# Six buffers for the first modulation rows, and weight sums moved ahead in a bidirectional scan layer

## The chip, the cores and the metric

The kernel runs on one core of a Trainium2 chip. The metric is the device time of one execution, in microseconds (us); each time shown is a median of several executions. Shares and rows come from one execution that the hardware profiler took.

## The reference

One layer of a diffusion backbone over 2176 tokens of width 1024: 128 context tokens and 2048 latent tokens, with different modulation vectors. The layer is, for both groups:

```python
mod = silu(c) @ w_mod + b_mod                       # 6 x 1024: shift1, scale1, gate1, shift2, scale2, gate2
h = rmsnorm(x, norm1) * (1 + scale1) + shift1
z = h @ w_in                                        # sc_b, sc_c, sc_x | q, k, v, o | gates
y_sc = sc_b * conv3(sc_c * sc_x)                    # short convolution, 512 wide
h_m = mlstm_bidir(q, k, v, gates, C0, n0, m0)       # 4 heads of 128, chunks of 128 tokens, both directions
h_m = headnorm(h_m) * sigmoid(o)
x = x + gate1 * (concat([y_sc, h_m]) @ w_out)
h2 = rmsnorm(x, norm2) * (1 + scale2) + shift2
a, g = split(conv3(h2 @ w_up))                      # 2 x 2816
x = x + gate2 * ((silu(g) * a) @ w_down)
y = rmsnorm(x, final_norm)
```

All arrays are float32. The kernel returns `y` for all tokens and the final scan states of the context tokens.

## The kernel before

Activations lie transposed: 128 features on the partitions, tokens along the free axis. A projection in float32 precision is made of three matmuls in a reduced format: each operand is split in a high part (made by ACT) and a low part (made by DVE as the rest), `wh`/`wl` for weights, `hH`/`hL` for activations, and `wh*hH`, `wh*hL`, `wl*hH` are added up in one PSUM bank. TensorE (PE) does the matmuls, ACT and DVE split operands and empty PSUM, and SyncE (SP) issues all transfers on one queue, in order. A scheduler puts the instructions of each engine in a fixed order, from the order in which the code is written and its own costs; pools of buffers (`bufs=n`) bound how far a load may run ahead. Each engine executes its own list in order.

The stages, in order of time:

1. First modulation. `mod_pe` loads one 128-wide row of `w_mod` (0.5 MB) and multiplies it with `silu(c)` on PE, 16 times: 8 rows of shift1 and 8 of scale1, in the order scale, shift, scale, shift. The rows go through two buffers `wst` and two `wsu`. Between them `raws(0)` loads the first 512-token block of x, and its squares are summed.
2. Values and gates of the last 1024 tokens (`vg_of`), whose normalized form is `gapply` (scale on DVE, shift and high part on ACT, low part on DVE). Each value weight is loaded through `wst` and split. Then the keys of these tokens (`key`), and `gsums`, which makes sums of activation quarters.
3. The pairs: the other projections of the last 1024 tokens, as ten 2x2 block products with seven products in place of eight (`pair_weights` makes the sums of weights, `pair` does 7 x 12 matmuls). After each of the seven products a generator is stepped (`side`); here that is `first_stats`, the sums of squares of the first 1152 tokens.
4. Values, gates and keys of the first 1152 tokens (`vg_first`, `heads`), and the scan's gate phase between the heads.
5. Scan sums. 34 units `Sums`, one for each chunk and pair of heads: two transposes of `k2` into `S`, a copy to `kT`, two matmuls `vw`x`kT` into `y`, and the running state `sb` from it by ACT and DVE. `weave` puts them between the heads of the projections q and o (`fill`).
6. The scan proper (`Mix`) with the short convolution and the output projection (`out_proj`) between, then the feed-forward layer: seven-product blocks over `w_up` and `w_down`.

Two pieces of work on DVE are put beside stages 4 and 5 as the generator `side`. `prep_down` loads blocks of `w_down`, makes the four sums that the last layer's seven products need, and stores them in `wD`: 12 steps of two loads, four operations and four stores. `mod_dve` computes the 32 other modulation rows on DVE, two reductions of 1024 columns for each. Both use the pool `wm`, four buffers. `side` is stepped once for each step of `vg_first`, of `heads`, and of the weave of the scan sums.

Buffers that the change touches: the pool `rp` (eight buffers of 384 columns, named `row`) takes evicted projection rows and the x rows that `out_proj` adds to; six more of 512 columns in the pool `sw` serve the pairs. The pool `xg` holds x of the second 512-token block and the values on their way out. In the order of instructions below a name ends in the number of its buffer.

Of the kernel before, what the change touches and what calls it, by code (L numbers as in the profile page):

```python
# [58 lines left out]
def hymba_kernel(ctx: ExitStack, tc: tile.TileContext, I, O):  # L59
# [302 lines left out]
    with ExitStack() as ph1:  # L362
# [5 lines left out]
        rp = ph1.enter_context(tc.tile_pool(name="rp", bufs=8))  # L368
# [36 lines left out]
        def head(w, b, h, hs, dst, func, scale):  # L405
            t0, n = BL[b]
            acc = gemm(w, hs[b], n)
            r = rp.tile([P, 384], F32, name="row")
# [68 lines left out]
        def out_proj(defer):  # L477
            def load_r(x):
                m, b = STEPS[x]
                t0, n = BL[b]  # L480
                xr = rp.tile([P, 384], F32, name="row")
                Q.dma_start(xr[:, :n], I["x"][m][:, t0:t0 + n])
                return xr
# [63 lines left out]
        with tc.tile_pool(name="ex", bufs=1, side="right") as ex, \  # L547
# [16 lines left out]
            def raws(blk):  # L564
                def get(pool, name, k0, n, bufs, w):
                    t = pool.tile([P, 4, 384] if w else [P, n, NG], F32, name=name, bufs=bufs)
# [75 lines left out]
            mods(2, 5)  # L642
            inv_rms(ss, NG, gcol(0))
            mods(5, 8)
            ws = load_vg(0)
# [26 lines left out]
            def key(w, h, blk):  # L672
# [24 lines left out]

            def row():
                return sw.tile([P, NG], F32, name="row", bufs=6)
# [178 lines left out]
        def prep_down():  # L878

            for mp in range(4):  # L880
                for c0 in range(0, KD, 512):
                    n = min(512, KD - c0)
                    a, b, s = (mp_.tile([P, 1024], F32, name="wm", bufs=4).rearrange("p (k c) -> p k c", k=2)[:, :, :n]
                               for _ in range(3))
                    for r, t in enumerate((a, b)):
                        Q.dma_start(t, I["w_down"][mp][:, r, :, c0:c0 + n])
                    yield
                    a11, a12, a21, a22 = a[:, 0], a[:, 1], b[:, 0], b[:, 1]
                    V.tensor_add(s[:, 0], a21, a22)
                    V.tensor_sub(s[:, 1], s[:, 0], a11)  # L890
                    V.tensor_sub(a12, a12, s[:, 1])
                    V.tensor_sub(a21, a11, a21)
                    for i, t in enumerate((s[:, 0], s[:, 1], a12, a21)):
                        Q.dma_start(wD[mp, i][:, c0:c0 + n], t)
                    yield

        side = chain(prep_down(), mod_dve())
# [277 lines left out]
        def weave(units, fill, blocks, side=None):  # L1175

            n = len(units)
            for i in range(-1, n + 3):
# [6 lines left out]
                for x in (0, 1) if i < 0 else (i + 2,):  # L1185
# [4 lines left out]
                if side:  # L1190
# [8 lines left out]
        for _ in vg_first():  # L1199
            next(third, None)  # L1200
            next(side, None)
        run(third)
        with tc.tile_pool(name="gt", bufs=1, side="right") as gt:
            gph = gate_phase()
            kh = heads(BA, hs, 16, kD, AF.Copy, 1.0)
            while True:
# [5 lines left out]
                run(islice(kh, 2), side)  # L1212
            run(kh, side)
# [387 lines left out]
```

## Time and profile before

| | |
|---|---|
| median of 3 runs | 2499.48 us (2497.95 to 2500.31) |
| profiled execution | 2498.36 us |
| its span, first to last instruction | 2496.4 us |
| PE busy | 2433.0 us (97%) |
| DVE busy | 1808.2 us (72%) |
| ACT busy | 1143.5 us (46%) |
| mean granted TensorE clock | 0.988 |
| DMA | 506.07 MB, mean 203 GB/s |

A row of the profile names the line, the engine, the operation, what is written and read, and its busy time; the time in brackets is how long the engine sat idle before it and which event ended that. PE is matmul time, PEld the weight loads that overlap it. Tables by stretch give the busy time of each engine in that stretch of the span, the granted clock as a share of full speed, the share of time in which DMA engines were busy, and GB/s. In a profile a buffer's number is left out, so `k2` reads `k`.

### The profile page before, as it was taken

What the parts mean: (1) busy time and instruction counts of PE and PEld (TensorE: products, weight loads), DVE (VectorE), ACT (ScalarE), POOL (GpSimd) and SP (SyncE); (2) the same over time, 40 slices, a digit from 0 to 9 for tenths busy, and PEclk for the clock granted to TensorE, in tenths of its full rate; (3) what the DMA queues carried; (4) which work ended last, traced back from release to release, by engine and by line L of the source; (5) the groups of instructions that cost most, each with busy time, mean ns of one, the idle gap of its engine ahead of it and who ended that gap; (6) DMA issues with size and microseconds to landing.
All of it is one profiled execution on the core that took longest, in us unless ns stands there. A gap on an engine that the chain in (4) does not pass through costs nothing.

```text
span 2496.4 us, 42843 instructions
## 1 busy us (share of the span) xinstructions
PE 2433.0 (97%) x16347; PEld 2325.2 (93%) x16347; DVE 1808.2 (72%) x3419; ACT 1143.5 (46%) x2170; POOL 66.7 (3%) x127
## 2 busy tenths in 40 slices
PE   7999999899999989999999999999999999999998
PEld 7988889788999989989999999999999988889998
DVE  4655675687566876789888888776767688677665
ACT  4533453233444543555455446554545454443343
POOL 0000000000011110000000000000000000000000
PEclk9999999899999999999999999999999999999999
DMA  7433169898866886877455446544444476576544
GB/s 268 140 108 116 60 196 306 275 295 275 249 196 211 272 275 201 276 248 254 156 189 210 155 146 229 199 147 168 147 169 146 164 277 231 190 276 204 180 156 149
DMA packets 250270, 506.07 MB, mean 203 GB/s; under 512 B 22850, under 2 KB 145874, under 8 KB 239186
## 3 DMA queue, kind: packets, MB, share of 16 engines
q1 hardware_dynamic: 250066, 503.35, 60.8%
q8 instruction: 128, 2.10, 0.3%
q14 instruction: 76, 0.62, 0.1%
HBM read 355.24 MB, written 148.03 MB: 202 GB/s over the span
## 4 chain that ended last, share of the span: by engine, by line
PE 57%; DMA 4%; DVE 4%; issue 1%; ACT 1%; SPq 0%; POOL 0%; DVEq 0%; ACTq 0%
PE pa L1440 7%; PE pa L1442 7%; PE pa L1441 7%; PE pb L1442 3%; PE pb L1440 3%; PE pb L1441 3%; PE pa L1498 2%; PE pa L1499 2%; PE pa L1500 2%; PE pc L1441 2%; PE pc L1442 2%; PE pc L1440 2%; PE pc L1498 2%; PE pc L1500 2%; PE pc L1499 2%; PE pb L1499 2%
## 5 line engine op out<-in xcount | busy, mean ns | idle before, releaser
L1440 PE MATMUL pa<-tH,wh 128*128 128x272 f32 x1408 | 409.1, 291 | 5.3 <-DVE row L499 4.2
L1442 PE MATMUL pa<-tH,wl 128*128 128x272 f32 x1408 | 407.9, 290 | 0.0
L1441 PE MATMUL pa<-tL,wh 128*128 128x272 f32 x1408 | 406.0, 288 | 0.3 <-DVE tL L280 0.3
L286 ACT ACTIVATE wh<-st 128x512 fp32r<-128x512 f32 (+1 forms) x312 | 189.4, 609 | 408.7 <-PE pa L1441 115.4
L213 PE MATMUL acc<-hH,wh 128*128 128x384 f32 (+1 forms) x960 | 329.4, 343 | 6.3 <-ACT wh L112 6.3
L215 PE MATMUL acc<-hH,wl 128*128 128x384 f32 (+1 forms) x960 | 322.9, 337 | 0.3 <-DVE wl L115 0.2
L214 PE MATMUL acc<-hL,wh 128*128 128x384 f32 (+1 forms) x960 | 322.9, 336 | 0.0
L287 DVE TENSOR_TENSOR wl<-st,wh 128x512 fp32r<-128x512 f32 (+1 forms) x312 | 205.3, 660 | 93.6 <-ACT wh L286 89.4
L1281 DVE SCALAR_TENSOR_TENSOR tt<-raw,fw,tt 128x127 f32<-128x127 f32 (+4 forms) x264 | 242.2, 947 | 41.9 <-ACT tt L1287 40.7
L1440 PEld LDWEIGHTS pa<-tH,wh 128*128 128x128 f32 x1408 | 265.7, 189 | 6.2 <-DVE row L499 4.2
L1441 PEld LDWEIGHTS pa<-tL,wh 128*128 128x128 f32 x1408 | 266.2, 189 | 0.5 <-DVE tL L280 0.5
L1442 PEld LDWEIGHTS pa<-tH,wl 128*128 128x128 f32 x1408 | 265.5, 189 | 0.0
L1440 PE MATMUL pb<-tH,wh 128*128 128x272 f32 x704 | 203.7, 289 | 0.4 <-ACT wh L286 0.4
L1442 PE MATMUL pb<-tH,wl 128*128 128x272 f32 x704 | 203.6, 289 | 0.0
L1441 PE MATMUL pb<-tL,wh 128*128 128x272 f32 x704 | 202.8, 288 | 0.0
L213 PEld LDWEIGHTS acc<-hH,wh 128*128 128x128 f32 x960 | 183.0, 191 | 9.2 <-ACT wh L112 8.4
L215 PEld LDWEIGHTS acc<-hH,wl 128*128 128x128 f32 x960 | 182.1, 190 | 1.9 <-DVE wl L115 1.2
L214 PEld LDWEIGHTS acc<-hL,wh 128*128 128x128 f32 x960 | 183.0, 191 | 0.7 <-issue 0.2
L286 ACT ACTIVATE wh<-s 128x512 fp32r<-128x512 f32 x176 | 110.9, 630 | 150.9 <-PE pc L1441 90.3
L287 DVE TENSOR_TENSOR wl<-s,wh 128x512 fp32r<-128x512 f32 x176 | 120.6, 686 | 33.1 <-ACT wh L286 29.3
L1440 PEld LDWEIGHTS pb<-tH,wh 128*128 128x128 f32 x704 | 132.4, 188 | 0.6 <-ACT wh L286 0.6
L1441 PEld LDWEIGHTS pb<-tL,wh 128*128 128x128 f32 x704 | 132.6, 188 | 0.0
(296 smaller groups left out, 5924.5 us busy)
## 6 DMA issues: line engine op xcount, KB each, us to landing
st<-in_w_up SPq DMA_DIRECT2D x88, 512.0 KB, 4.6
wU<-s SPq DMA_DIRECT2D x22, 1024.0 KB, 7.0
s<-wU SPq DMA_DIRECT2D x22, 1024.0 KB, 5.9
st<-wD SPq DMA_DIRECT2D x32, 704.0 KB, 4.9
st<-in_w_down SPq DMA_DIRECT2D x28, 704.0 KB, 5.3
wst<-in_w_in SPq DMA_DIRECT2D x38, 512.0 KB, 5.1
R<-nD SPq DMA_DIRECT2D x34, 512.0 KB, 5.6
wm<-in_w_modr SPq DMA_DIRECT2D x32, 512.0 KB, 5.1
```

The costliest lines, as they stand in the source:

```text
L213: PE.matmul(acc[:, :n], w_h, hH[:, k, :n], start=(k == 0), stop=False)
L214: PE.matmul(acc[:, :n], w_h, hL[:, k, :n], start=False, stop=False)
L215: mm = PE.matmul(acc[:, :n], w_l, hH[:, k, :n], start=False, stop=(k == KT - 1))
L286: S.activation(wh[:, :n], a, AF.Copy)
L287: V.tensor_sub(wl[:, :n], a, wh[:, :n].bitcast(F32))
L1281: V.scalar_tensor_tensor(o, i, w, o, op0=ALU.mult, op1=ALU.add)
L1440: PE.matmul(acc, wh[:, w], rh, start=(kk == 0 and i in (0, 1, 5)), stop=False, skip_group_check=True)
L1441: PE.matmul(acc, wh[:, w], rl, start=False, stop=False, skip_group_check=True)
L1442: mm = PE.matmul(acc, wl[:, w], rh, start=False, stop=(kk == 3), skip_group_check=True)
L1498: PE.matmul(acc[p], wh[:, k], th[:, t], start=(c == kk == 0), stop=False, skip_group_check=True)
L1499: PE.matmul(acc[p], wh[:, k], tl[:, t], start=False, stop=False, skip_group_check=True)
L1500: PE.matmul(acc[p], wl[:, k], th[:, t], start=False, stop=(c == 2 and kk == nk - 1), skip_group_check=True)
```

## The change

- The first modulation rows go through six buffers in turn, two `wsu` and the four of `xg`; `wst` is left to the value weights, of which the first two are loaded and split between the rows. The second x block is loaded into `xg` after the rows; the last two k-tiles of the first block have a buffer `xh` of their own.
- `prep_down` moves beside the pairs, with three buffers `wm` in the pool `sw` and its sums in a buffer `xt`; it is spread over four steps of `side` for each block. `side` is stepped after every product of the pairs.
- `mod_dve` alone is left beside stages 4 and 5, and is stepped on every second step.
- The scan sums' loads stand three units ahead in the code (two before).
- `row` is one pool for all its users: six buffers of 512 columns. A key is evicted and stored in one piece of 512 columns, not two of 256.

```diff
+    def row():
+        return rp.tile([P, 512], F32, name="row")
...
-        rp = ph1.enter_context(tc.tile_pool(name="rp", bufs=8))
+        rp = ph1.enter_context(tc.tile_pool(name="rp", bufs=6))
...
-                    return get(xp, "xt", 0, 3, 2, 1) + get(xp, "xt", 3, 3, 2, 1) + get(xg, "xg", 6, 2, 5, 0)
-                return [x for k in range(0, KT, 2) for x in get(xg, "xg", k, 2, 5, 0)]
+                    return get(xp, "xt", 0, 3, 2) + get(xp, "xt", 3, 3, 2) + get(xg, "xh", 6, 2, 1)
+                return [x for k in range(0, KT, 2) for x in get(xg, "xg", k, 2, 4)]
...
+            homes6 = cycle("uuxxxx")
+
             def mod_pe(mt):
-                if mt < 8:
-                    st = wp.tile([P, WN], F32, name="wst", bufs=2)
+                if next(homes6) == "u":
+                    st = ex.tile([P, WN], F32, name="wsu", bufs=2)
                 else:
-                    st = ex.tile([P, WN], F32, name="wsu", bufs=2)
+                    st = xg.tile([P, 2, NG], F32, name="xg", bufs=4).rearrange("p k t -> p (k t)")
...
-            mods(2, 5)
+            mods(2, 4)
+            ws = load_vg(0)
             inv_rms(ss, NG, gcol(0))
-            mods(5, 8)
-            ws = load_vg(0)
+            mods(4, 8)
             run(gapply(0, x1))
...
-                for i in range(2):
-                    r = rp.tile([P, 384], F32, name="row")[:, :256]
-                    S.activation(r, acc[:, i * 256:(i + 1) * 256], AF.Copy)
-                    Q.dma_start(kD[h][:, TG + blk * NG + i * 256:TG + blk * NG + (i + 1) * 256], r)
+                r = row()
+                S.activation(r, acc, AF.Copy)
+                Q.dma_start(kD[h][:, TG + blk * NG:TG + (blk + 1) * NG], r)
...
-            side = first_stats()
+            side = chain(first_stats(), prep_down())
             for x, p in enumerate(PAIRS):
                 if x < len(PAIRS) - 1:
-                    run(gpair(*p), side if x > 2 else None, 3)
+                    run(gpair(*p), side)
...
-        side = chain(prep_down(), mod_dve())
+        side = mod_dve()
...
-        for _ in vg_first():
+        for x, _ in enumerate(vg_first()):
             next(third, None)
-            next(side, None)
+            if x % 2:
+                next(side, None)
...
-                for x in (0, 1) if i < 0 else (i + 2,):
+                for x in range(lead) if i < 0 else (i + lead,):
...
-                if side:
+                if side and i % 2:
                     next(side, None)
...
-        weave([Sums(c, hp) for c in range(NL - 1, -2, -1) for hp in range(2)], fill, (1, 0, 1), side)
+        weave([Sums(c, hp) for c in range(NL - 1, -2, -1) for hp in range(2)], fill, (1, 0, 1), 3, side)
```

`prep_down` in its new place, with a pause between its two halves and an empty step behind them:

```python
def prep_down():
    for mp in range(4):
        for c0 in range(0, KD, 512):
            n = min(512, KD - c0)
            a, b = (sw.tile([P, 1024], F32, name="wm", bufs=3).rearrange("p (k c) -> p k c", k=2)[:, :, :n]
                    for _ in range(2))
            s = xp.tile([P, 4, 384], F32, name="xt").rearrange("p k t -> p (k t)")[:, :2 * n]
            ...
            yield
            ...                                      # two sums into s
            yield
            ...                                      # two sums in place, four stores to wD
            yield
            yield
```

The first place is SP's list in the first modulation. Before, from the first x block on (`wsu`, `wst`: rows of `w_mod`; `xt`, `xg_210`: x of the first block; `xg_458`: of the second):

```order
L568 DMA xt_206<-in_x 128x3x512
L568 DMA xt_208<-in_x 128x3x512
L568 DMA xg_210<-in_x 128x2x512
L620 DMA wsu_235<-in_w_mod 128x1024
L620 DMA wst_247<-in_w_mod 128x1024
L620 DMA wsu_260<-in_w_mod 128x1024
L620 DMA wst_272<-in_w_mod 128x1024
L648 DMA bgate_132<-in_b_gate 128x16
L568 DMA xg_458<-in_x 128x2x512
L620 DMA wsu_285<-in_w_mod 128x1024
```

After, from the same place (`xg_235` and the like are rows of `w_mod` now, `wst` the value weights):

```order
L571 DMA xt_206<-in_x 128x3x512
L571 DMA xt_208<-in_x 128x3x512
L571 DMA xh_210<-in_x 128x2x512
L625 DMA xg_235<-in_w_mod 128x1024
L625 DMA xg_247<-in_w_mod 128x1024
L625 DMA wsu_260<-in_w_mod 128x1024
L625 DMA wsu_272<-in_w_mod 128x1024
L110 DMA wst_285<-in_w_vg 128x1056
L110 DMA wst_292<-in_w_vg 128x1056
L625 DMA xg_306<-in_w_mod 128x1024
```

Two value weights come in between the rows, and the second block's x goes behind the last row.

The second place is SP's list at the first loads of the scan sums (`k2`, `v2`). Before, they follow the last stores of keys (`kD`) and of the down weights' sums (`wD`):

```order
L410 DMA kD_63<-row_4227 128x384
L410 DMA kD_63<-row_4262 128x384
L868 DMA wm_4039<-in_w_modr 128x1024
L894 DMA wD_76<-wm_3902 128x384 x2
L894 DMA wD_76<-wm_3900 128x384
L894 DMA wD_76<-wm_3901 128x384
L1036 DMA k2_4277<-kD_63 128x2x128
L1041 DMA v2_4279<-vD_66 128x258
L1036 DMA k2_4281<-kD_63 128x2x128
```

After, they stand among the stores of the values (`vD`) of the stage before, ahead of all stores of keys of the first 1152 tokens:

```order
L403 DMA vD_66<-rv_3412 128x258
L1223 DMA sb_4314<-in_state 128x2x129
L1041 DMA k2_4316<-kD_63 128x2x128
L1046 DMA v2_4318<-vD_66 128x258
L892 DMA wm_3528<-in_w_modr 128x1024
L403 DMA vD_66<-rv_3445 128x258
L1041 DMA k2_4320<-kD_63 128x2x128
L1046 DMA v2_4322<-vD_66 128x258
L1041 DMA k2_4324<-kD_63 128x2x128
```

The loads moved ahead by the whole stage of keys, and the down weights' stores are gone from it.

The third place is DVE's list in the pairs, between two half weights (`wl`). Before, at the second pair's convolution:

```order
L729 TENSOR_TENSOR wl_1575<-wsu_1324,wh_1574 128x512
L798 SCALAR_TENSOR_TENSOR yr_1496<-row_1474,scw_133,yr_1496 128x8x63
L800 SCALAR_TENSOR_TENSOR yr_1496<-row_1474,scw_133,yr_1496 128x8x63
L729 TENSOR_TENSOR wl_1596<-wst_1476,wh_1595 128x512
L722 TENSOR_TENSOR wst_1476<-wst_1476,wsu_1477 128x512
```

After, at the same convolution (`wm`, `xt`: the down weights and their sums, lines 852 to 856):

```order
L730 TENSOR_TENSOR wl_1668<-wsu_1303,wh_1667 128x512
L801 SCALAR_TENSOR_TENSOR yr_1571<-row_1543,scw_133,yr_1571 128x8x63
L717 TENSOR_TENSOR s_1689<-wsu_1552 128x512
L852 TENSOR_TENSOR xt_1664<-wm_1663 128x512
L719 TENSOR_TENSOR s_1689<-s_1689,wst_1551 128x512
L853 TENSOR_TENSOR xt_1664<-xt_1664,wm_1662 128x512
L730 TENSOR_TENSOR wl_1691<-wst_1551,wh_1690 128x512
L855 TENSOR_TENSOR wm_1662<-wm_1662,xt_1664 128x512
L856 TENSOR_TENSOR wm_1663<-wm_1662,wm_1663 128x512
```

The four sums of a down block stand between the pair's own sums and the low parts of its weights.

More of the change, by code (lines that the diff above doesn't have):

```diff
@@ L480, in load_r @@
                 t0, n = BL[b]
-                xr = rp.tile([P, 384], F32, name="row")
+                xr = row()
                 Q.dma_start(xr[:, :n], I["x"][m][:, t0:t0 + n])
@@ L876, in mod_dve @@
                 yield
[L878 to L895, printed above, removed]
-        side = chain(prep_down(), mod_dve())
+        side = mod_dve()
         WG, EM, AC = range(3)
@@ L1173, in third, with weave @@
                 Q.dma_start(yD[4 + 2 * hp:6 + 2 * hp, :, t0:t0 + P].rearrange("h d t -> d h t"), o2)
-        def weave(units, fill, blocks, side=None):
+        def weave(units, fill, blocks, lead, side=None):
             n = len(units)
@@ L1211, in hymba_kernel @@
                     break
-                run(islice(kh, 2), side)
-            run(kh, side)
+                run(islice(kh, 2), side, 2)
+            run(kh, side, 2)
         sbs, sfs = [], []
@@ L1243, in hymba_kernel @@
             sfs.append(sf)
-        weave([Mix(c, hp) for c in range(-1, NL) for hp in range(2)], fill, (2, 1, 2))
+        weave([Mix(c, hp) for c in range(-1, NL) for hp in range(2)], fill, (2, 1, 2), 2)
         phr.close()
```

26 lines of the change are left out of this document (21 added, 5 removed).

## The prediction

> **What bounds the kernel now.** I read the page's first lines, then the busy time by stretch, then each stretch in which TensorE (PE) is not full, in order of time.
>
> ```profile
> span 2496.4 us, 42843 instructions
> ...
> PE 2433.0 (97%) x16347; PEld 2325.2 (93%) x16347; DVE 1808.2 (72%) x3419; ACT 1143.5 (46%) x2170; POOL 66.7 (3%) x127
> ```
>
> PE is busy 97% of the span, so only the 63 us in which it idles, and the stretches at a lower clock, can be won. The next view gives stretches of the span in us: length, busy time of each engine, granted clock, DMA share.
>
> ```profile
> core 0: us, PE busy (x) PEld busy (x) DVE busy (x) ACT busy (x) POOL busy (x), PEclk, DMA share, GB/s
> 0.00:43.03 43.03, 34.11 (x266) 33.82 (x267) 11.69 (x37) 9.41 (x16) 1.40 (x9) 0.96 0.86 302
> 43.03:61.60 18.57, 14.29 (x97) 13.80 (x96) 16.59 (x28) 15.02 (x25) 0.00 (x0) 0.82 0.60 200
> 131.00:330.00 199.00, 199.00 (x874) 162.14 (x873) 114.59 (x183) 74.78 (x133) 3.31 (x3) 1.00 0.28 93
> 352.00:400.00 48.00, 47.34 (x381) 46.93 (x382) 30.75 (x77) 19.58 (x40) 1.43 (x14) 1.00 0.88 291
> 400.00:457.70 57.70, 54.97 (x308) 51.69 (x306) 31.82 (x93) 17.98 (x35) 0.00 (x0) 0.97 0.90 299
> 457.70:478.30 20.60, 10.83 (x29) 8.24 (x30) 14.84 (x30) 3.32 (x8) 0.00 (x0) 0.59 0.87 271
> 478.30:628.80 150.50, 140.27 (x754) 129.56 (x753) 119.20 (x253) 51.06 (x133) 0.00 (x0) 0.98 0.91 280
> 628.80:1070.00 441.20, 433.54 (x2796) 431.69 (x2795) 314.64 (x909) 199.91 (x535) 47.44 (x72) 0.99 0.76 242
> 1100.00:2480.00 1380.00, 1377.36 (x10066) 1336.30 (x10065) 1060.00 (x1630) 682.30 (x1110) 7.51 (x8) 1.00 0.55 189
> ```
>
> In order: the modulation rows; the first value and gate matmuls up to their first eviction; the seven-product pairs (PE full, DMA a quarter busy); the first blocks' values and gates; the keys; the scan sums, as two rows; the scan proper with the output projection; the feed-forward layer. From 628.80 on the order of PE's matmuls is the same in both kernels but for two transposes, and PE is 98% busy or more, so I take the change to act only before 628.80. There PE is short in two places: the first 62 us, and 457.70 to 628.80, where DMA is 0.87 to 0.91 busy.
>
> **First modulation rows.** The rows are from the order of instructions by time: start, duration, and in brackets the idle time and its releaser. One row of `w_mod` is 16 records.
>
> ```profile
> 13.54 1.95 PE L623 MATMUL acc<-csil,wst 128*128 128x128 f32 x16
> ...
> 17.64 3.59 PE L623 MATMUL acc<-csil,wsu 128*128 128x128 f32 x16 [2.15 <-DMA wsu<-in_w_mod]
> ...
> 22.86 1.95 PE L623 MATMUL acc<-csil,wsu 128*128 128x128 f32 x16
> ...
> 24.65 1.95 PE L623 MATMUL acc<-csil,wst 128*128 128x128 f32 x16
> ...
> 30.01 0.95 PE L129 MATMUL st<-ones,ss 128*128 128x1 f32 x8
> ...
> 41.01 2.02 PE L623 MATMUL acc<-csil,wst 128*128 128x128 f32 x16 [1.02 <-DMA wst<-in_w_mod]
> ...
> 44.96 1.33 DVE L115 TENSOR_TENSOR wl<-wst,wh 128x528 fp32r<-128x528 f32 x2
> ...
> 46.89 0.39 PE L394 MATMUL acc<-wh,hH 128*128 128x264 f32 x1 [2.96 <-ACT hH L591]
> ```
>
> A row takes 24.65 - 22.86 = 1.79 us. The fourth starts at 13.54; twelve more and the 0.95 of the squares' sum would end at 13.54 + 13 x 1.79 + 0.95 = 37.8. Now the last ends at 41.01 + 2.02 = 43.03. The 5.2 us between are waits for rows that could not be loaded before a buffer came free, and one row at half clock (3.59). With six buffers, rows 5 and 6 are issued right behind the first block of x, with no wait for PE; of the rest, a load stands two to four rows ahead. The x loads of the second block move behind the last row, two of them, 1.0 MB, now issue ahead of it. Unknown is whether the DMA engines keep up: sixteen rows of 0.52 MB, 2.1 MB of x and two value pieces are 11.6 MB; at the 302 GB/s of 0 to 43.03 they land at 38.4 and the last row ends near 40.3 (gain 2.8); but that rate holds pauses in which SP waited for a buffer, and the stretch below shows 419 GB/s. So the gain is 2.8 to 5.2; I take 5.0, near the end that rests on the busy rate. Loading x later costs nothing: block 0's value and gate matmuls cover it (192 matmuls, over 20 us).
>
> After that the value weights no longer wait for a row's buffer: two of their four splits (L115, 1.33 us a pair on DVE, in the middle of the chain from scale to `hH`) go ahead of it. DVE is busy 16.59 of 18.57 us there, so I take 1.5 us, between 0 (ACT, 15.02, is nearly as full) and 3.4 (half of 6.7 us at half clock below).
>
> The clock by stretch:
>
> ```profile
> 15.50:17.60 2.10, 0.00 (x0) 0.00 (x0) 1.86 (x4) 1.06 (x2) 0.00 (x0) 0.98 1.03 419
> 17.60:21.00 3.40, 3.36 (x16) 3.39 (x17) 2.98 (x5) 2.10 (x4) 0.00 (x0) 0.51 1.04 398
> ...
> 48.30:55.00 6.70, 5.38 (x25) 5.08 (x24) 6.68 (x11) 6.70 (x13) 0.00 (x0) 0.50 0.87 295
> ```
>
> An idle stretch of 2.1 us was followed by 3.4 us at 0.51, one of 2.96 us by 6.7 us at 0.50. The idle stretch ahead of the first value matmul stays (spread, scale, `hH`), so I leave its half clock in. [...]
>
> **Scan sums.**
>
> ```profile
> 458.25 0.35 SPq L410 DMA_DIRECT2D kD<-row  x1
> ...
> 461.23 0.69 SPq L1036 DMA_DIRECT2D k<-kD  x1
> ```
>
> ```profile
> 465.21 0.69 PE L1058 MATMUL S<-ident,k 128*128 128x128 f32 x2 [7.51 <-DMA k<-kD]
> ...
> 612.72 0.34 PE L215 MATMUL acc<-hH,wl 128*128 128x384 f32 x1
> ...
> 615.88 0.34 PE L215 MATMUL acc<-hH,wl 128*128 128x384 f32 x1
> 616.05 0.38 PE L1058 MATMUL S<-ident,k 128*128 128x128 f32 x2
> ...
> 617.15 0.38 PE L1058 MATMUL S<-ident,k 128*128 128x128 f32 x2
> ...
> 628.45 0.53 PE L213 MATMUL acc<-hH,wh 128*128 128x384 f32 x1
> ```
>
> The last sums end at 628.45, 170.7 us after 457.70. In between lie 24 projection heads of 24 matmuls and 34 sums. A matmul takes (615.88 - 612.72) / 18 = 0.175 us, a unit of sums 617.15 - 616.05 = 1.10 us: 576 x 0.175 + 34 x 1.10 = 138.2. So 32.5 us are lost, more than PE's idle time shows, since half clock lies in it (0.59 in the first row). The waits there, in all, times, longest:
>
> ```profile
> PE S L1058 <- DMA k<-kD: 8.8, 2, 7.5
> PE acc L213 <- ACT wh L112: 6.3, 4, 2.4
> PE y L1069 <- DVE sb L1083: 2.4, 3, 1.2
> ...
> ACT wh L112 <- DMA wst<-in_w_in: 13.7, 10, 2.7
> ...
> L872 DVE SCALAR_TENSOR_TENSOR wm<-wm,cB 128x1024 f32<-128x1024 f32 x64 | 78.1, 1220 | 13.1 <-DMA wm<-in_w_modr 9.0 <-DMA wD<-wm 3.6
> ```
>
> The longest goes: the first `k2` load was issued at 461.23, behind the stores of the keys and of the last down weights; now four stand ahead of those stores, and a head's matmuls follow the first transposes. The heads' weights waited on DMA; all 64 of the reductions (78.1 us of DVE, 16.8 MB of loads) stood in this stage, 28 are left. DVE's 134 us here fall by 36 x 1.22 = 44; DMA falls by 9 MB of reduction rows and the last down weights. What is late next is PSUM turnover, where a sum's matmul waits for `sb` and the next transposes for `kT`: 2.4 us and little more now, with reductions queued between; I leave 6 us in all, as DVE stays dense in the first half. Gain 26.5. Bounds: the weights' waits and two half-clock stretches stay (6.3 + 2 x 1.7, with the 2.4 and 1.0 to 2 us of turnover, some 14 left: gain 18.5), or nothing is lost (32.5).
>
> **Down weights beside the pairs, and the reductions ahead.**
>
> ```profile
> DVE wm L889 <- DMA wm<-in_w_down: 25.2, 10, 4.6
> ```
>
> ```profile
> L889 DVE TENSOR_TENSOR wm<-wm x12: 557/692/693, 356.3 to 458.2; 128x512 f32<-128x512 f32 x8, 128x384 f32<-128x384 f32 x4
> ```
>
> ```profile
> ACT wh L728 <- PE acc L763: 34.4, 18, 2.6
> ```
>
> The 48 operations are 32 x 0.69 + 16 x 0.56 = 31 us of DVE, moved to the pairs: 114.6 + 31 = 146 of 199 us. Their 24 loads and 48 stores (23 MB) lift DMA there by some 115 GB/s, on 93. PE pays nothing as long as DVE delivers the `wl` of a half weight and the evictions; ACT waits for PE there, that is, weights stand ready as far as the buffers reach. Cost 0, bounds 0 and the rival's price. In the place left, 352 to 457.70, 36 reductions (44 us of DVE) replace 31 us, and the DMA load falls by about a third (some 20 MB go, 9 MB come, of 31). DVE gets 62.6 - 31 + 44 = 76 of 106 us, tight in the 20 us where the last gates are evicted; the scan's gate chain is in its queue. I charge 1.5 us (bounds: gain 1.8, loss 4).
>
> **Rows and stores.** Rows share six buffers in place of eight and six; keys are evicted and stored once in place of twice (eight evictions and issues fewer). In the output projection a row's load now waits for the store three steps back.
>
> ```profile
> L482 SPq EVENT_SEMAPHORE x35: 17/17/4401, 850.7 to 1045.7; - x35
> ```
>
> SP waits for buffers there already, once 4.4 us, with weight loads and stores queued behind, and PE is 98% busy; loads still run three steps ahead. Cost 0, bounds 0 and 3 us.
>
> **Sum.** -5.0 - 1.5 - 26.5 + 1.5 + 0 = -31.5: span 2464.9, the profiled execution 2498.36 - 31.5 = 2466.9. It stood 1.1 us under the median of the runs; against the 2499.48 the prediction is 2468.
>
> **Rivals.**
> *Half the gain.* The sums are bound by what follows a product: `S` has one buffer, `y` three, and each unit needs ACT and DVE in turn. For it: DVE is 119 of 150 us busy, and the waits for `sb` and `kT` are there. Against it: at 616.05 two units ran back to back in 1.10 us each with no wait. Then between 12 and 18.5 us go in that stage: 2476 to 2483.
> *Slower: DVE blocked in the pairs.* Each of the 12 steps needs two loads; where one is late, DVE stands with `wl` and the eviction of a bank behind it, and PE reuses that bank one product (12 matmuls) later. DVE waited 25.2 us in 10 such waits before. If each of 24 loads cost PE 2.5 us the pairs would be 60 us longer: 2528. It decides the sign from 1.3 us a load. Against it: in 352 to 457.70, with DMA 0.9 busy, those waits left PE 47.34 of 48 us busy, and DMA is 0.28 busy in the pairs. [...]
> *It does not do what it says in the first stage:* DMA stays the limit there; 2.2 us of gain less, inside the range.
>
> **Chances.** The forecast (2457 to 2475) 0.72; half the gain, 2475 to 2486, 0.18; slower 0.04; a loss elsewhere that eats most or all of it, 0.06. The range leaves out the slower cases and the far ends: 2457 to 2484. A change of 0.2% (5 us) is about what this kernel's runs can tell from none. Faster 0.92, same 0.04, slower 0.04.
>
> **What would show it.** Right: the last modulation row ends near 38, the first eviction of gates near 55; PE full from 131 to 330 of the old time with DVE near 73%; the first scan sums' transposes with no wait for `k`; that stage near 144 us long, with no stretch below full clock; everything after it as long as before. Wrong: PE waits for `wl` or for a bank in the pairs, for gates or `ls` at the keys, or for `y` in the sums.

## The result, and the profile after

The changed kernel takes 2476.95 us in the median of four runs, the kernel before 2498.72: a ratio of 0.992, with a 95% interval of 0.9902 to 0.9938. That is 22 us less; I had forecast 31.5 us less (2468). In a later measurement the ratio was 0.990 (0.9879 to 0.992). Single runs of either kernel scatter by some 5 us around the median, so differences of 2 or 3 us between kernels are read below from stages of the traces, not from the medians.

The first lines of the page after (its profiled execution took 2481.01 us, the longest of the four):

```profile
span 2479.2 us, 42907 instructions
...
PE 2427.5 (98%) x16347; PEld 2322.7 (94%) x16347; DVE 1806.6 (73%) x3419; ACT 1146.3 (46%) x2166; POOL 65.4 (3%) x127
```

The work of PE and DVE is the same; what shrank is PE's idle time, from 63 to 52 us, and the time at half clock (the mean granted clock rose from 0.988 to 0.991). Busy time by stretch, in the same columns as before (length; PE, weight loads, DVE, ACT, POOL; granted clock, DMA share, GB/s):

```profile
0.00:41.83 41.83, 32.95 (x266) 32.82 (x267) 13.20 (x39) 11.28 (x15) 1.39 (x9) 0.96 0.89 332
131.00:330.00 199.00, 198.08 (x864) 160.11 (x863) 136.19 (x227) 72.48 (x125) 3.74 (x7) 1.00 0.59 201
400.00:459.90 59.90, 55.34 (x307) 52.21 (x306) 52.60 (x142) 18.43 (x38) 0.00 (x0) 0.94 0.61 199
459.90:480.00 20.10, 19.16 (x111) 18.24 (x109) 15.87 (x35) 6.40 (x16) 0.00 (x0) 1.00 0.78 242
480.00:604.77 124.77, 120.68 (x674) 113.86 (x674) 63.43 (x137) 53.40 (x141) 0.00 (x0) 1.00 0.81 244
604.77:1054.60 449.83, 436.83 (x2802) 434.18 (x2801) 315.59 (x910) 196.52 (x524) 46.06 (x72) 0.98 0.74 231
```

The reader is to see three things. The scan sums, from the end of the keys to the last sum, take 20.10 + 124.77 = 144.9 us at full clock, where they took 171.1, about a seventh of it at half clock (0.93 granted on the mean). The pairs (second row) are no longer full, 198.08 of 199 us. And the scan proper with the output projection (last row) has grown. Its stretch starts where the last sum ends and reaches a little past the end of the row before: the matmul that starts at 1070.0 before starts at 1051.45 now, so 441.2 us have become 446.7.

The stages side by side, from PE's matmuls in each trace, in us ("again" is a second measurement of the changed kernel, told below). The last value matmul is taken at its start. "Scan proper" here is the time from the start of its first to that of its last product of `k` with `q`:

| stage | before | after | again |
|---|---|---|---|
| start to first pair | 144.9 | 143.0 | 141.5 |
| pairs | 198.0 | 200.2 | 200.0 |
| first blocks' values | 54.2 | 53.8 | 53.9 |
| last value matmul to last scan sum | 231.7 | 207.8 | 208.0 |
| scan proper | 321.3 | 325.2 | 325.2 |
| the rest, to PE's last matmul | 1539.5 | 1542.5 | 1537.4 |
| PE's last matmul | 2489.7 | 2472.5 | 2466.0 |

The rest (with the 16.6 us between the sums and the scan proper) differs by 5 us between two executions of the same kernel; nothing is read into that.

### The profile page after: what moved, and what is told of

Same layout as the page of the kernel before. It is cut to its first block, busy times and chain, and to the rows that moved or that the text cites. A ratio compares the mean times of both kernels' runs of the same rounds, so it can differ in the third digit from the quotient of the medians.

```text
span 2479.2 us, 42907 instructions
## 1 busy us (share of the span) xinstructions
PE 2427.5 (98%) x16347; PEld 2322.7 (94%) x16347; DVE 1806.6 (73%) x3419; ACT 1146.3 (46%) x2166; POOL 65.4 (3%) x127
## 4 chain that ended last, share of the span: by engine, by line
PE 78%; DMA 11%; DVE 7%; issue 2%; ACT 1%; SPq 1%; POOL 0%; DVEq 0%; ACTq 0%; POOLq 0%
PE pa L1446 7%; PE pa L1448 7%; PE pa L1447 7%; PE acc L216 4%; PE acc L218 4%; PE acc L217 4%; PE pb L1448 3%; PE pb L1446 3%; PE pb L1447 3%; PE pa L1505 2%; PE pa L1504 2%; PE pa L1506 2%; PE pc L1446 2%; PE pc L1448 2%; PE pc L1447 2%; DMA wm<-in_w_modr 2%
## 5 line engine op out<-in xcount | busy, mean ns | idle before, releaser
L218 PE MATMUL acc<-hH,wl 128*128 128x384 f32 (+1 forms) x960 | 322.0, 335 | 0.0
```

The source lines that it names most:

```text
L218: mm = PE.matmul(acc[:, :n], w_l, hH[:, k, :n], start=False, stop=(k == KT - 1))
```

## Experiments

Each edit is shown against the changed kernel unless the text says otherwise.

**The first stage alone.** The kernel before with the new homes of the modulation rows, the new order of x, rows and value weights, and nothing else:

```diff
-                if mt < 8:
-                    st = wp.tile([P, WN], F32, name="wst", bufs=2)
+                if next(homes6) == "u":
+                    st = ex.tile([P, WN], F32, name="wsu", bufs=2)
                 else:
-                    st = ex.tile([P, WN], F32, name="wsu", bufs=2)
+                    st = xg.tile([P, 2, NG], F32, name="xg", bufs=4).rearrange("p k t -> p (k t)")
...
-            mods(2, 5)
-            inv_rms(ss, NG, gcol(0))
-            mods(5, 8)
-            ws = load_vg(0)
+            mods(2, 4)
+            ws = load_vg(0)
+            inv_rms(ss, NG, gcol(0))
+            mods(4, 8)
```

> Theory (the DMA engines were the limit at row 5, not the buffers): the first stage ends as in the changed kernel, the last modulation row near 41.8 us and the first pair 1.9 us earlier than before, and the whole kernel is 1 to 3 us under the 2498.7 of the kernel before. Rival (the prediction's term: only buffers held the rows back, and the one profile of the changed kernel was unlucky): the last row ends near 38, and the kernel is 6 to 7 us under the one before.

Measured: the last row ends at 40.3 us, the first pair starts 3.5 us earlier than before, and the pairs take 198.0 us. The median is 2498.02 against 2499.91, a ratio of 0.9994 (0.9982 to 1.0006). That is between the two expectations. The stage gains 3.5 of the 6.5 us that the sum forecast for it, and the whole time cannot tell it from nothing. The reason stands in the changed kernel's trace. First SP's issues, of the fifth row before, and of x and the fifth and sixth row after; then PE after; then two stretches after:

```profile
9.53 0.34 SPq L620 DMA_DIRECT2D wsu<-in_w_mod  x1
```

```profile
4.47 1.19 SPq L571 DMA_DIRECT2D xt<-in_x  x2
5.71 0.64 SPq L571 DMA_DIRECT2D xh<-in_x  x1
6.40 1.86 SPq L625 DMA_DIRECT2D xg<-in_w_mod  x2
```

```profile
10.74 3.62 PE L628 MATMUL acc<-csil,xg 128*128 128x128 f32 x31
17.64 5.44 PE L628 MATMUL acc<-csil,xg 128*128 128x128 f32 x32 [3.27 <-DVE ss L590]
```

```profile
14.40:17.60 3.20, 0.00 (x0) 0.00 (x0) 2.88 (x5) 2.02 (x4) 0.00 (x0) 1.00 1.04 408
18.74:22.15 3.41, 3.41 (x19) 3.41 (x18) 1.54 (x4) 0.33 (x1) 0.00 (x0) 0.50 1.03 418
```

The fifth row is issued 3.1 us earlier than before, and PE starts on it at 17.64, as in the kernel before. The DMA engines are full in the wait, at 408 GB/s, with 2.1 MB of x issued ahead of the row. (The page puts the wait down to a sum of squares on DVE that ended at 17.61, which these matmuls do not read. The last part of the row landed at 17.50 by its semaphore, and in four other kernels with this order the trace names the row's load at this place.) From 18.74 on 3.41 us of the next rows run at half clock.

**x between the rows.** If that reading is right, the row must come earlier when x doesn't stand in front of it. Here `part_in` loads k-tiles 0 to 2, then 3 to 5, then 6 and 7, and `part_sq` squares and adds them. The edit also puts the scale (`inv_rms`) nearer to the last rows in the code:

```diff
-            x1 = raws(0)
-            ss = gsquares(x1)
-            mods(2, 4)
-            ws = load_vg(0)
-            inv_rms(ss, NG, gcol(0))
-            mods(4, 8)
+            mods(2, 3)
+            part_in()
+            mods(3, 4)
+            part_in()
+            part_sq(0, 3)
+            mods(4, 5)
+            part_in()
+            part_sq(3, 6)
+            mods(5, 6)
+            part_sq(6, 8)
+            ws = load_vg(0)
+            mods(6, 7)
+            inv_rms(ss, NG, gcol(0))
+            mods(7, 8)
```

> The x of the first block is loaded in three parts, behind rows 6, 8 and 10, in place of whole behind row 4. Theory (row 5 waited because 2.1 MB of x shared the DMA engines with it): the 3.3-us gap ahead of row 5 and the half clock behind it go, the last row ends at 37 to 38 and the kernel takes 2471 to 2474. Rival (the rate of the DMA engines is the limit in any order): the gap moves to a later row, the last row ends at 41 or later, and the kernel is at 2476 or more.

The same stretch, and the first 40.52 us:

```profile
0.00:40.52 40.52, 32.75 (x274) 32.70 (x275) 16.61 (x45) 13.88 (x21) 1.79 (x9) 1.00 0.86 319
14.40:17.60 3.20, 3.20 (x31) 3.20 (x31) 0.57 (x4) 1.67 (x3) 0.00 (x0) 1.00 1.03 410
```

The gap is gone at the same rate of the DMA engines (410 GB/s), and no half clock is recorded in the stage (1.00 in the first row). The last row ends at 40.5, not 37 to 38: the first rows start later with six of them in flight (at 6.02 us, 5.61 in the changed kernel), and PE waits 1.7 us for the scale (`rc` on POOL), which now stands ahead of the last rows. But behind the last row the first value matmul starts at once, at 40.3 (46.9 before, 45.4 after), and the first pair starts 9.1 us earlier than before. The order of the bytes held the fifth row, not the buffers and not the rate alone. How much of the rest belongs to the order of x, and how much to the scale that now stands before the last rows, this run does not separate. The median is 2473.84, a ratio of 0.9898 (0.9879 to 0.9917): of the 7.1 us that the first pair gains on the changed kernel the median shows 3, which the scatter does not separate from none. In this execution the stretch from the last value matmul to the last sum was 4.8 us longer (212.6).

**The down weights' sums back in their place,** with the reductions stepped as before (`prep_down` itself and the steps beside the keys, the pairs and the scan sums go back too):

```diff
-            side = chain(first_stats(), prep_down())
+            side = first_stats()
...
-        side = mod_dve()
+        side = chain(prep_down(), mod_dve())
...
-            if x % 2:
-                next(side, None)
+            next(side, None)
```

> Theory (moving the down weights' sums, with the reductions that this lets run earlier, is what made the scan-sums stage shorter): with both put back the stage from the last head of the keys to the last sum is 165 to 171 us again, its first load stands behind stores again, the pairs lose their extra 2 us, and the kernel takes 2494 to 2499. Rival (the loads three ahead did most of it): the stage stays under 152 us and the kernel under 2484.

Measured: from the last value matmul to the last sum 234.4 us (231.7 before, 207.8 after); from the end of the keys to the last sum 172.4, as expected within 1.4 us; the pairs 198.0; the median 2503.69 against 2499.91, a ratio of 1.0015 (1.0002 to 1.0028). That is above the 2494 to 2499 expected: this kernel keeps the six row buffers, and its scan proper took 326.4 us. PE's waits in the stage of the sums, after, and with the sums put back:

```profile
PE y L1074 <- DVE sb L1088: 2.8, 3, 1.2
PE S L1063 <- ACT kT L1065: 2.2, 2, 1.8
```

```profile
PE S L1059 <- DMA k<-kD: 8.1, 1, 8.1
PE y L1070 <- DVE sb L1084: 5.2, 5, 2.3
PE y L1070 <- DVE vw L1063: 4.8, 4, 2.5
```

After, no wait for `k` is left, as forecast, and the two kinds that follow a product come to 5.0 us. With the sums back, the wait for the first `k` stands there again, although loads are three ahead. All of the gain of that stage hangs on the moved sums and on the reductions that run earlier because of them. How it divides between the queue's order, DVE's shorter list (79.3 us of work in the stage, 134.0 before and with the sums back) and the lighter load of the DMA engines (0.80, 0.90) was not tested.

**Loads two ahead.**

```diff
-(1, 0, 1), 3, side)
+(1, 0, 1), 2, side)
```

> Theory (the third load ahead adds nothing once the stores no longer stand in front): the stage takes 144 to 147 us and the kernel 2476 to 2479. Rival (the lead hides the DMA latency): waits for k of 5 us or more come back and the kernel is 2483 or more.

207.0 us from the last value matmul to the last sum, 2477.37 in the median: the third load ahead adds nothing.

**Reductions not spread.**

```diff
-            if x % 2:
-                next(side, None)
+            next(side, None)
...
-                run(islice(kh, 2), side, 2)
-            run(kh, side, 2)
+                run(islice(kh, 2), side)
+            run(kh, side)
...
-                if side and i % 2:
+                if side:
```

> The reductions are stepped at every step again, the down weights' sums stay beside the pairs. Theory (moving the sums made the gain, and spreading the reductions only moves DVE work between a stage with a margin and one without): the scan sums' stage is 0 to 3 us shorter, the values, gates and keys 1 to 5 us longer, the kernel within 3 us of 2477. Rival (spreading is what keeps DVE from stalling PE before the scan): values, gates and keys 8 us or more longer, the kernel at 2482 or more.

The first blocks' values take 59.2 us (53.8 after), with one wait of 3.1 us for a split of `hL` on DVE and the clock at 0.94; from the last value matmul to the last sum it is 209.8 (207.8). Together 7.4 us more, up to the last sum. From the last pair to the end of the keys it is 7.2 us more, between the two expectations, and the sums' stage itself did not get shorter by having fewer reductions. But the median is 2478.37, as the theory said and not separable from the changed kernel's. So in this one execution spreading belongs to the gain; the medians do not show it.

**No reductions stepped in the gate chain.**

```diff
-                if side and i % 2:
+                if side and (i % 2 or i < 10):
...
-                run(islice(kh, 2), side, 2)
+                run(islice(kh, 2))
```

> No reductions are stepped between the last value block and the end of the gate chain; they run in the first ten turns of the scan sums instead. Theory (two reductions and what queues behind them on DVE make the gates' transposes late, and PE's idle time of 3.4 us there is followed by half clock): the transposes come 9 us or less after the last value matmul (12.3 in the changed kernel), the half clock from 407.9 to 414.7 goes, the scan sums' stage grows by 2 us at most, and the kernel takes 2471 to 2475. Rival (ACT's exponential and logarithm set the time): the transposes still come 11 us or more after, and the kernel takes 2476 or more.

The gates' first transpose, before and after, then what DVE does ahead of `fc` after, and the stretch there:

```profile
406.19 0.33 PE L959 MATMUL S<-ident,fc 128*128 128x128 f32 x1 [0.23 <-DVE fc L952]
```

```profile
409.19 0.47 PE L964 MATMUL S<-ident,fc 128*128 128x128 f32 x1 [3.39 <-DVE fc L957]
```

```profile
403.17 1.22 DVE L896 SCALAR_TENSOR_TENSOR wm<-wm,cB 128x1024 f32<-128x1024 f32 x1
...
404.32 0.30 DVE L954 SCALAR_TENSOR_TENSOR fe<-fc 128x136 f32<-128x136 f32 x1
...
408.83 0.30 DVE L957 SCALAR_TENSOR_TENSOR fc<-fc,fe 128x136 f32<-128x136 f32 x1 [1.75 <-ACT fe L956]
```

```profile
407.86:414.70 6.84, 5.51 (x18) 5.10 (x19) 5.64 (x18) 1.31 (x3) 0.00 (x0) 0.50 0.87 279
```

The reduction in the first of DVE's rows, with two more from 399.03 on, makes `fe` late: it starts 7.4 us after the last value matmul. Behind it `fc` waits for ACT. With the edit `fe` starts 3.9 us after that matmul, and the transposes come 8.7 us after it (12.3 after, 9.1 before), as the theory said. But a longer wait at the second transpose, for DVE's copy of the first, takes the place of the old one (it was 1.8 us before the change):

```profile
PE S L964 <- DVE ls L965: 3.2, 1, 3.2
```

and part of the half clock stays (a granted clock of 0.93 from 404.9 to 411 us and of 0.69 from 411 to 415). From the last value matmul to the last sum it is 204.8 us, 3.0 less than after; the median is 2475.03, a ratio of 0.9891 (0.9866 to 0.9916), not separable from the changed kernel's. The transposes came as expected; the half clock did not go.

**The down weights' loads two steps ahead of their sums.**

```diff
                             Q.dma_start(t, I["w_down"][mp][:, r, :, c0:c0 + n])
                         yield
+                        yield
...
                             Q.dma_start(wD[mp, i][:, c0:c0 + n], t)
                         yield
-                        yield
```

> In the pairs the two loads of down weights get two steps, not one, before their sums, and the stores one, not two. Theory (DVE stands in the sums' wait for these loads, 22.6 us in 7 waits, with the evictions of the banks behind it, and PE loses 2.2 to 3.2 us): the five stalls of 0.2 to 1.7 us at the pairs' ends shrink, the pairs lose 1 us at most against the kernel before, and the kernel is 1 to 2 us shorter. Rival (the stores hold the buffers, so that the loads are issued as late as now): the waits and the stalls stay as they are.

DVE's waits for these loads fall from 21.8 us to 10.8, the pairs take 199.1 us. That is no verdict: the unaltered order took 198.7 to 201.4 us in the other kernels here, and with this edit in the combination below the pairs took 200.9, with DVE's waits at 12.0 us. The median is 2477.41. The next experiment takes the loads away.

**The down weights loaded once.**

```diff
+                ta, tb = (sw.tile([P, 1024], F32, name=f"w{i}") for i in "ab")
+                for r, t in enumerate((ta, tb)):
+                    Q.dma_start(t.rearrange("p (k c) -> p k c", k=2), I["w_down"][0][:, r, :, :512])
...
-                        a, b = (sw.tile([P, 1024], F32, name="wm", bufs=3)...
-                                for _ in range(2))
+                        a, b, o = (t.rearrange("p (k c) -> p k c", k=2)[:, :, :n]
+                                   for t in (ta, tb, sw.tile([P, 1024], F32, name="wm")))
-                        for r, t in enumerate((a, b)):
-                            Q.dma_start(t, I["w_down"][mp][:, r, :, c0:c0 + n])
                         yield
...
-                        V.tensor_sub(a12, a12, s[:, 1])
-                        V.tensor_sub(a21, a11, a21)
+                        V.tensor_sub(o[:, 0], a12, s[:, 1])
+                        V.tensor_sub(o[:, 1], a11, a21)
...
```

This kernel leaves out all loads of down weights but the first two, so that the last layer works with other weights.

> Beside the pairs only the first two loads of down weights are made; all twelve steps do their sums on these and store them, so the down weights that later stages read are other ones. DVE has the same work and the same stores, but waits for no load after the first. Theory (DVE standing in these waits, with the evictions behind it, is what costs the pairs 0.7 to 3.4 us): the pairs take 198.0 to 198.5 us, with no stall of PE over 0.4 us for an eviction. Rival (31 us more of DVE work makes the evictions late by itself): 199 us or more.

The waits in the pairs after (DVE's longest, and all of PE's), then the pairs' whole stretch after and with this edit:

```profile
DVE xt L852 <- DMA wm<-in_w_down: 21.8, 7, 6.7
```

```profile
PE acc L763 <- DVE row L826: 0.4, 1, 0.4
PE acc L763 <- DVE row L782: 0.3, 1, 0.3
PE acc L763 <- DVE row L811: 0.2, 1, 0.2
```

```profile
142.97:343.18 200.21, 199.29 (x873) 161.24 (x872) 144.95 (x255) 79.09 (x144) 3.74 (x7) 1.00 0.58 195
```

```profile
138.81:336.73 197.92, 197.92 (x873) 161.44 (x872) 144.58 (x254) 79.27 (x144) 3.75 (x7) 1.00 0.42 146
```

DVE does the same 144.6 us of work, and PE is full again: 197.92 us, as before the change. So DVE's work is free here, and the 2.2 us that PE loses in the changed kernel come with the loads (only 0.9 of it shows as waits, the rest as matmuls that start late). That they come from DVE standing in the wait for a load, with the eviction of a bank behind it, is argued, not shown: PE's releasers, the evictions, speak for it, but the run without the loads also moves a quarter less by DMA, so contention is not excluded, and halving the waits gave 199.1 us once and 200.9 the other time. The kernel took 2468.33 us in its one execution, at a mean granted clock of 0.993 (0.991 in the profiled execution after), so its whole time says nothing on the pairs.

**Rows two ahead.** In the scan proper the queue of DMA issues waits more often for a row's buffer than before (29 times, 15 before).

```diff
-            rows = [load_r(x) for x in range(3)]
+            rows = [load_r(x) for x in range(2)]
...
-                if x + 3 < len(STEPS):
-                    rows.append(load_r(x + 3))
+                if x + 2 < len(STEPS):
+                    rows.append(load_r(x + 2))
```

> In the output projection rows are loaded two steps ahead, not three, so that a load waits for the store four steps back. Theory (with six buffers the load of a row blocks the queue of DMA issues until a store has landed, 56.6 us in 29 waits against 24.3 in 11 before, and the loads of R behind it make DVE and PE late): the waits halve, the gap of 2 to 3 us at the first output rows goes, and the stretch from the first to the last transposed product of the scan proper takes 321 to 323 us, not 324 to 325; the kernel is 2 to 3 us shorter. Rival (the gap comes from the order in which weights and R arrive, not from the rows): the waits halve and the stretch stays at 324 or more.

The waits fell to 37.4 us in 21, but the scan proper took 324.9 us, with a gap of 4.5 us. The theory's fix failed. SP's queue in the changed kernel, at the gap, shows why:

```profile
850.93 0.61 SPq L504 DMA_DIRECT2D xD<-row  x1
855.56 0.33 SPq L485 DMA_DIRECT2D row<-in_x  x1
855.99 0.39 SPq L1178 DMA_DIRECT2D yD<-o  x1
856.46 0.42 SPq L1110 DMA_DIRECT2D R<-nD  x1
```

The row's load directly follows a store and waits for it to land (4.0 us), and `R`, which the next product needs, is issued only behind it. With rows two ahead the same place reads alike: the store at 848.58, the row at 853.52, `R` at 854.42. The order of the queue is made when the program is built, and it moves a load up to where its buffer should be free.

**R ahead of the rows.** So here the order was held as well:

```diff
+                with tc.issue_after(lastR[0].ins):
+                    Q.dma_start(xr[:, :n], I["x"][m][:, t0:t0 + n])
```

together with rows two ahead, where `lastR` is the latest load of `R`.

> Rows two ahead, and in the queue of DMA issues each row's load comes after the load of R that is traced ahead of it. Theory (in the first scan-proper steps the load of R stands behind a row's load that waits 4 to 5 us for a store): the gap of 2 to 4.5 us ahead of the transposed product there falls to 1.5 us or less, and the stretch from the first to the last transposed product takes 321 to 323 us. Rival (DVE and the output weights are late there whatever the queue's order): the gap stays at 2 us or more, the stretch at 324 or more.

SP's waits for stores ahead of a row's load from 600 to 1060 us, before, after, and here; then PE's waits in the scan proper, before, after, and here:

```profile
SPq L482 <- DMA xD<-row: 30.6, 15, 4.4
```

```profile
SPq L485 <- DMA xD<-row: 56.6, 29, 5.1
```

```profile
SPq L490 <- DMA xD<-row: 21.1, 13, 3.1
```

```profile
PE st L129 <- DVE o L1170: 4.1, 1, 4.1
PE st L1168 <- DVE rc L132: 1.6, 2, 1.1
PE S L1116 <- DVE R L1125: 1.2, 1, 1.2
```

```profile
PE st L129 <- DVE o L1175: 4.6, 1, 4.6
PE S L1121 <- DVE R L1130: 3.1, 1, 3.1
PE st L1173 <- DVE rc L132: 1.1, 1, 1.1
```

```profile
PE S L1126 <- DVE R L1135: 3.1, 1, 3.1
PE st L1178 <- DVE rc L132: 2.8, 1, 2.8
PE st L129 <- DVE o L1180: 1.8, 1, 1.8
```

The stretch takes 321.7 us, as before the change (321.3), where the changed kernel and its other variants with six row buffers took 323.8 to 326.4 (the kernel with the sums back is the 326.4; the kernel with the first stage alone, which keeps eight, took 322.0). A wait of 3.1 us for `R` is still there, 30 us earlier, where the theory had 1.5 or less, and other waits are shorter. So the stretches bear out that six row buffers, with the queue in this order, cost 3 to 4 us in this stage. Which of PE's waits pays for it differs from kernel to kernel, and I leave that open. The medians of these two kernels, 2478.15 and 2478.23, are too scattered to show 3 us.

**Again, and three repairs together.** Last come the changed kernel itself once more, and a kernel with x between the rows, no reductions stepped in the gate chain, and the down weights' loads two steps ahead.

> The changed kernel once more, unaltered. Theory (the losses at the gates, in the pairs and in the scan proper belong to the kernel and not to one execution): the pairs take 199.7 to 200.7 us, the gates' transposes come 11.5 to 13 us after the last value matmul, the scan proper takes 324 to 326 us; the last modulation row ends between 40 and 42. Rival (the profiled execution was an odd one): two or more of these three are within 0.5 us of the kernel before (198.0, 9.1, 321.3).

> The x of the first block in three parts between the rows, no reductions in the gate chain, the down weights' loads two steps ahead. Theory (the three losses are separate and add): 7 us at the first pair, 1 us in the pairs, 3 to 4 us at the gates less than the changed kernel: 2466 to 2470. Rival (what is won early is given back in a later stage, as the 7 us of x between the rows shrank to 3 in the medians): 2471 to 2475.

Again: pairs 200.0, transposes 12.0 us after the last value matmul, scan proper 325.2. All three losses belong to the kernel and not to one execution; the last row ended at 42.2, just outside what was expected. The repaired kernel takes 2467.42 us in the median, a ratio of 0.9873 (0.9853 to 0.9893) to the kernel before; the changed kernel measured beside it takes 2475.42, 8 us more. In its trace the first pair starts at 135.9 (141.5 again), the last value matmul to the last sum takes 204.9 (208.0), and the pairs 200.9: two of the repairs add, the third does nothing.

## Why the prediction was right, and where its sum was not

The time lies in the range, and the chance went to the right side. But 2476.95 is 2 us outside the band that I gave the forecast itself (2457 to 2475, 0.72) and inside the one of the half-gain rival, so it is the width of the range that holds it. The term that carries the forecast was right to half a microsecond in the first execution and to 2 us in the second, and several small terms, nearly all on the optimistic side, took some 10 us from the sum. By its steps, from the profiled executions (after; again):

- *Scan sums, -26.5.* The stage took 144.9; 146.6 us, against 171.1 before: 26.2; 24.5 less. No wait for `k`, and 5.0; 5.6 us of waits for turnover where I had left 6 in all: as forecast. The clock was full in the first execution, with 3.4 us at half clock in the second. Of the 64 reductions only 21; 20 were left behind the keys, where I had 28. Putting the sums back undoes the gain, loads two ahead do not.
- *Down weights beside the pairs, 0.* Measured +2.2; +2.0. The step that failed is "PE pays nothing": I had the load about right (201 GB/s in the second row above, on 93 before; I expected 115 more), and DVE's work is free, but the loads are not. The likely way, not shown, is the rival's: DVE blocked by a load with evictions behind it, at 0.1 us for each of 24 loads in place of the 1.3 that would have turned the sign.
- *Keys and gates, +1.5.* From the last pair to the end of the keys' heads +1.9; +0.5 (114.8 to 116.7; 115.3 us), in the bounds. The gates' transposes are 3.2 us later after the last value matmul, as the text had feared for the gate chain.
- *First modulation rows, -5.0.* The last row ended 1.2; 0.8 us earlier. The step that failed is the choice "near the end that rests on the busy rate". The rate was as assumed, above 400 GB/s. What was left out is the order. The fifth row, issued behind 2.1 MB of x, started at 17.64 us whether its load was issued at 9.53 or at 6.40, so the 2.15 us that I had read as a wait for a buffer were a wait for these bytes. In the first execution the gap of 3.27 us and the half clock behind it (1.7 us) take back 5.0 us, and 1.2 are left because the fourth row ended 1.1 us earlier. The rival "DMA stays the limit there" was the right one for this term, with 3.8 us of gain less in place of 2.2.
- *From the last row to the first gates, -1.5.* Measured -0.7; -2.5 from the last row to the first pair. The first eviction of gates came at 56.35; 56.48, 5.2; 5.1 us earlier than before where 6.5 was forecast, and half clock ahead of it fell from 6.8 to 3.4 us. Part of this is given back: PE itself is 4.0; 3.9 us ahead at that place, and in the first execution a second stretch of half clock, from 63.11 to 66.52, follows. At the first pair 1.9; 3.4 us are left of the 6.5.
- *Rows and stores, 0 with a bound of 3.* Measured +3.9; +3.9 in the scan proper, just outside. The reason for 0, "SP waits for buffers there already", was the reason to charge something: those waits went from 30.6 to 56.6; 47.5 us from the sums to the end of the projection.
- *Everything after as long as before* held for the feed-forward layer as far as two executions can tell (+3.0; -2.1 with all that follows the scan proper).

The sum of these in the profiled executions is -17.2; -23.6, and -21.8 by the medians. The half-gain rival is not what happened, though the time lies in its band: the stage that it spoke of gained what was forecast, to 2 us.

## What to carry to other kernels

Work that sits in a full stage is worth moving to one with idle engines, and its engine time there can be free, as the down weights' sums were (pairs of 197.92 us with 144.6 us of DVE's work in them, and 197.97 with 120.4 before); price instead what its loads bring: traffic for the DMA engines (195 GB/s in the pairs after, 146 without the loads), and waits in the queue of DMA issues, where here `R` stood behind the 4.0 us that a row's load waited for a store. For a load that is to come earlier, count the bytes that are issued ahead of it, not the buffers: the earlier issue here, behind DMA engines that were already full (408 GB/s), gained nothing: the row started at 17.64 us either way. When buffers are shared or cut, look at what the queue does while it waits for one, and look at the order that the built program gives it.

## What the runs showed of the hardware

Half clock does not follow from the length of a gap alone. PE idle for 2.1 us in the kernel before was followed by 3.4 us at 0.51, and for 3.27 us in the changed one by 3.41 us at 0.50, both shown above. In the changed kernel the gap of 2.63 us ahead of the first value matmul, at 45.36, was followed by 3.41 us at 0.50 too. But in the kernel with the first stage alone, 2.54 us without PE work at the place of the first two (4.00 less 1.46 in the first row) left the clock at full speed:

```profile
14.00:18.00 4.00, 1.46 (x14) 1.30 (x13) 2.49 (x5) 2.19 (x5) 0.00 (x0) 1.00 1.04 412
18.00:22.00 4.00, 4.00 (x38) 4.00 (x37) 3.00 (x7) 1.53 (x3) 0.00 (x0) 1.00 1.03 416
```

So in these traces half clock came after the shorter gap of 2.1 us and not after the longer one of 2.54. A gap followed by 3.41 us at 0.50 costs 1.7 us more than it shows (an estimate, half of the 3.41), which accounts for part of the difference between executions: with the same order of loads and rows, the last row ended at 40.3 us in the kernel with the first stage alone, which had a clock of 1.00 up to 41 us, and at 41.8 in the changed one, which had 3.41 us at 0.50.
